# Output gate by tanh, and other places and load orders in the first projections of a hybrid mLSTM / MLA block

## The chip, the cores and the metric

One core of a Trainium2 chip runs the whole block in one launch. The metric is the device time in microseconds (us) of one execution; the median of several runs is given.

## The reference, cut to what matters

A sequence of 2048 tokens with 1024 features goes through one encoder layer. Beside the query and key columns the input projection gives the values, the output gate `o_pre`, the mLSTM gates, the compressed queries `c_q` (256 columns), the compressed keys `c_kv` (128) and the rotary keys (64).

```python
xn = rms_norm(h, ln_mix_g[l])
proj = xn @ w_in[l]
# mLSTM group: forward and backward chunkwise recurrence, then
h = rms_norm(h_fwd + h_bwd, norm_g)          # by head
y_a = sigmoid(o_pre) * h
# MLA group
q  = (rms_norm(c_q, q_norm_g) @ w_uq)        # 4 heads: 128 + 64 (rope)
kv = (rms_norm(c_kv, kv_norm_g) @ w_ukv)
y_b = softmax((q_nope k_nope^T + rope(q_rope) rope(k_rope)^T) * scale) @ v
h = h + concat(y_a, y_b) @ w_out             # then a conv-gated FFN, a gated
                                             # per-layer input and a final norm
```

## The kernel before, in words

The class `Block` runs the stages one after the other: the input projection (`in_proj`), attention with the mLSTM running beside it (`attend` over `mlstm`), the output projection, the FFN, the per-layer input and the final norm. All products are fp32 made of three fp32r passes: each operand is split into a high part (a cast on ScalarE, line 119) and a low part (a subtraction on VectorE, line 122), and `mm3` (line 132) multiplies high by high, high by low and low by high.

Tiles live in SBUF places with names: "w...", "x...", "t...", "s...". `self.at(place, ...)` puts a new tile into a place, and the first instruction that writes the new tile waits for the last reader of the old one. Only TensorE's order is written by hand. ScalarE, VectorE, GpSimd and SyncE get their order from a scheduler, and each works strictly in that order, so that an instruction that waits holds up all behind it. Almost all loads and stores are issued by SyncE (SP).

`in_proj` has three parts.

1. *The rest columns*, 0 to about 100 us: 16 row tiles `st` of 128 tokens. `load_x` (line 220) loads the transposed tile x_t, `load_rows` (line 225) the same rows untransposed, x_r, into two places in turn, for the sum of squares (`ssq_x`). `split_x` makes xh and xl; the product with the weights wsp gives 464 columns, from which come the gates gt (line 249, with the bias bg), the raw rows rs (line 252), the norms nn (lines 265 and 266, with gn) and the rows of compressed queries and keys, which are turned and stored in `rest_d` in DRAM. At `st` 10, `absorb_load` loads the turned up-projections of queries and keys into w8 and t6.
2. *The value columns*, about 100 to 263 us: 16 tiles of eight steps. A step is three matmuls, one with an xl and two with an xh (bk<-wsp,xl and bk<-wsp,xh). After each step `beside()` runs pieces of side work: the mLSTM gates in every third step, 1.4 pieces a step from the chain `absorb()` then `q_up()`, and from step 68 on every second step `raised`, which forms sums of x (xs, xsum) and splits them (op) for the third part.
   - `absorb()` multiplies the query up-projection by the key up-projection (gb<-ukvt,uqt), and for each head h the value up-projection by that head's 128 rows of w_out (gb<-woa,uvs); the result woo goes to `wo_d`. The raw rows wor have one place, w11; the next head's are loaded when this head's are split. There are six pauses (of one piece each) between split and product.
   - `q_up()` loads the compressed queries from `rest_d`, four of the eight column groups c of 256 tokens at a time (qraw, 1 MB, x11 and then x5), splits a group into cq in w8, multiplies by the up-projection (qpr<-wqo,cq for the rotary part, gb<-cq,wqn for the other), rotates (qtt, qro), splits (qsr) and turns (L788). w8 also holds the woo of `absorb`.
3. *Query, key and output-gate columns in pairs* (Winograd form), about 263 to 498 us. `finish()` applies Silu to the queries (line 582 for the convolved ones) and Sigmoid to the output gate (line 564, tiles uv and ug), and stores the gate in `o_d`.

`attend` starts within the last pair: score products into bk (lines 1135 to 1139), maxima (line 1140), exp (line 1158, pe), turning (line 1198, tb), and the split of the turned probabilities (pt). Exp and Sigmoid, and Exp and Silu, need different tables on ScalarE; a change is an ACT_TABLE_LOAD. The mLSTM beside it ends each chunk with line 1103: the turned tile (mb) times the output gate (og).

Of the kernel before, what the change touches and what calls it, by code (L numbers as in the profile page):

```python
# [11 lines left out]
F32R = mybir.dt.float32r  # L12
BF16 = mybir.dt.bfloat16
AF = mybir.ActivationFunctionType
ALU = mybir.AluOpType
# [4 lines left out]
P = 128  # L20
S = 2048
D = 1024
KT = D // P
NT = S // P
# [18 lines left out]
def pause(n):  # L43

    for _ in range(n):
        yield
# [14 lines left out]
class Block:  # L61
# [120 lines left out]
    def in_proj(self):  # L182
# [38 lines left out]
            return t  # L221

        def load_rows(st):
            t = self.at(("w13", "u2")[st % 2], [P, D], name="x_r")
            nc.sync.dma_start(t, d["x"][0, st * P:(st + 1) * P, :])
            return t

# [85 lines left out]
        with self.tc.manual_schedule(engines={ET.PE}):  # L313
            for st in range(NT + LAG_X + 1):
                if st + 2 < NT:
                    xq[st + 2] = load_x(st + 2)
                if st == 0:
                    rq[1] = load_rows(1)
                if st == 10:
                    self.absorb_load()  # L320
                if 14 <= st < 17:
                    vraw.append(load_raw(st - 14, OFF_V, 512, f"w{st - 4}"))
                if st == 0:
                    gn = self.at("t5", [P, 384], name="gn")
                    self.row_bcast(gn[:, 0:256], d["q_norm_g"][0], 256)
                    self.row_bcast(gn[:, 256:384], d["kv_norm_g"][0], 128)
                    bg = self.bg = self.row_bcast(self.cst.tile([P, 16], F32, name="bg"), d["b_gates"][0], 16)
                if 1 <= st < NT:
                    split_x(st, xq.pop(st))
                if 0 <= st - 1 < NT:  # L330
                    ssq_x(st - 1, rq.pop(st - 1))
                    if st + 1 < NT:
                        rq[st + 1] = load_rows(st + 1)
                if st == NT:
                    vws = split_raw(vraw[0], 512, VT)
                if 0 <= st - LAG_X - 1 < NT:
                    nq[st - LAG_X - 1] = norm_rest(st - LAG_X - 1, *sq.pop(st - LAG_X - 1))
                if 0 <= st - LAG_X < NT:
                    sq[st - LAG_X] = rest(st - LAG_X)
                if 0 <= st - LAG_X - 1 - LAG_R < NT:  # L340
                    turn_rest(st - LAG_X - 1 - LAG_R, nq.pop(st - LAG_X - 1 - LAG_R))

        cols = self.cst.tile([P, 8], F32, name="cols")
        self.gmix, ng = cols[:, 0:4], cols[:, 4:8]
        nc.sync.dma_start(self.gmix, d["gm_turned"])

        H = S // 2
        NAMES = ("B11", "T1", "T2", "B21", "T3", "T4", "B22")
# [52 lines left out]
            ws += split_raw(vraw[k2], 512, VT[2 * k2:])  # L401
        gates, raised = self.gates(), highs()
        side = chain(self.absorb(), self.q_up())
        when = [0, 0.0, False]

        def beside():

            n = when[0]
            when[0] += 1
            if n in (3, 8):  # L410
                turn_rest(NT - 2 + n // 8, nq.pop(NT - 2 + n // 8))
            if n >= 12 and n % 3 == 0:
                next(gates, None)
            if n >= 4:
                when[1] += self.VRATE
                while when[1] >= 1:
                    if next(side, self) is self and not when[2]:
                        when[2] = True
                        self.in_load(0)
                    when[1] -= 1  # L420
            if n == 10:
                pr = self.pml.tile([NT, P], F32, name="rps", tag="ml")
                nc.tensor.transpose(pr, rcol, self.ident)
                rr = self.at("s2", [NT, P], name="rrow")
                nc.vector.tensor_copy(rr, pr)
                nc.sync.dma_start(self.r_d.rearrange("(t p) -> t p", p=P), rr)
            if n >= 68 and n % 2 == 1 and (n < 82 or when[2]):
                next(raised, None)

        with self.tc.manual_schedule(engines={ET.PE}):  # L430
# [86 lines left out]
    def in_pairs(self, high, cwt, rrow, gcol, ng, row):  # L517
# [42 lines left out]
        def finish(s, half):  # L560
            u, c0 = (s.ug, s.uv)[half], 0 if s.i >= 6 else 8
            if s.kind == "o":
                t = u[:, 1:1 + H]
                nc.scalar.activation(t, t, AF.Sigmoid)
                dst = self.o_d[c0:c0 + 8, :, 2 * s.j + half, :]
            else:
                ct = s.j + 4 * half
                nc.vector.memset(u[:, 0:1], 0.0)
                if c0:
                    nc.vector.memset(u[:, H + 1:H + 2], 0.0)  # L570
                    nc.vector.tensor_copy(ehi[:, ct:ct + 1], u[:, 1:2])
                else:
                    nc.vector.tensor_copy(u[:, H + 1:H + 2], ehi[:, ct:ct + 1])
                    nc.vector.tensor_copy(elo[:, ct:ct + 1], u[:, H:H + 1])
                t = self.at(("w7", "w11")[half], [P, H], name="ct")
                nc.scalar.activation(t, u[:, 0:H], AF.Identity, bias=cwt[:, 3, ct:ct + 1], scale=cwt[:, 0, ct:ct + 1])
                for tap in (1, 2):
                    nc.vector.scalar_tensor_tensor(t, u[:, tap:tap + H], cwt[:, tap, ct:ct + 1], t,
                                                   op0=ALU.mult, op1=ALU.add)
                if c0:  # L580
                    nc.vector.tensor_copy(pa[:, ct:ct + 1], t[:, 0:1])
                nc.scalar.activation(t, t, AF.Silu)
                dst = self.qk_d[c0:c0 + 8, :, ct, :]
# [137 lines left out]
    def absorb(self):  # L721
# [9 lines left out]
            self.wqr.append(r)  # L731

        def load(h):
            r = self.at("w11", [P, D], name="wor")
            nc.sync.dma_start(r, d["w_out"][0, 512 + h * P:512 + (h + 1) * P, :])
            return r

        raw = load(0)
        yield from pause(5)
        for kt in range(2):  # L740
            ps = self.gbank([P, NH, P])
# [3 lines left out]
            yield  # L745
        for h in range(NH):
            wh, wl = [self.at(t, [P, D], F32R, "woa") for t in ("w12", "w10")]
            self.split(raw, wh, wl)
            if h + 1 < NH:
                raw = load(h + 1)  # L750
            us = self.at(f"s{h % 2}", [P, 2, P], F32R, "uvs")
            self.split(uv[:, h], us[:, 0], us[:, 1])
            yield from pause(6)
            o = self.at("w8", [P, D], name="woo")
            for hf in range(2):
                fs = slice(hf * 512, hf * 512 + 512)
# [7 lines left out]
    def q_up(self):  # L764
# [8 lines left out]
        raws, tables, old = {}, {}, None  # L773

        def load(c):
            raws[c // 4] = self.at(("x11", "x5")[c // 4], [P, 2, 1024], name="qraw")
            nc.sync.dma_start(raws[c // 4], self.rest_d[:, 0:2, c * 256:c * 256 + 1024])

        def table(c):
            tables[c // 2] = self.at(f"s{c // 2 % 3}", [P, 4, 2, 32], name="qcs")  # L780
# [18 lines left out]
        yield from pause(4)  # L799
        sr2 = self.at("x13", [P, 2, 2, NH, P], name="qsr")  # L800
        for c in range(8):
            cc = self.at("w8", [P, 2, 2, 256], F32R, "cq")
            o = c % 4 * 256
            self.split(raws[c // 4][:, :, o:o + 256], cc[:, 0], cc[:, 1])
            if c == 2:
                load(4)
            cs = tables[c // 2][:, c % 2 * 2:c % 2 * 2 + 2]
            ch, cl = cc[:, 0], cc[:, 1]
            yield from pause(1 if c else 7)
# [148 lines left out]
    def mlstm(self):  # L958
# [60 lines left out]
        for c in range(NT):  # L1019
# [80 lines left out]
            pt = mbank([P, NH, P])  # L1100
            for h in range(NH):
                nc.tensor.transpose(pt[:, h, :], hh[:, h, :], self.ident)
            nc.vector.tensor_tensor(hy[:, 1], pt, og, op=ALU.mult)
            nc.sync.dma_start(self.y_d[c, :, 0:4, :], hy[:, 1])
            yield

# [1056 lines left out]
```

## Time and profile before

| | |
|---|---|
| time before, median of 3 runs | 2942.8 us (2942.41 to 2944.44) |
| the profiled execution's own time | 2938.07 us |
| its span | 2936.1 us |
| mean granted TensorE clock | 0.995 |
| instructions | 40731 |
| moved by DMA | 530.19 MB, 181 GB/s on average |

How to read it: a line of the page or of a view gives the engine (PE is the matmul unit, PEld its weight loads, DVE VectorE, ACT ScalarE, POOL GpSimd, SP SyncE, SPq its DMA queue), the line of the kernel, the operation, the output and the inputs, the shape, and times in us. In brackets stands how long the engine was idle before, and what released it. PEclk is the clock granted to TensorE, 1.00 being full speed.

### The profile page before, as it was taken

Reading aid. Unit: us, or ns where it says so; the run is one execution under the profiler, and the core shown is the slowest. Engines: PE = TensorE matmul, PEld = TensorE weight load, DVE = VectorE, ACT = ScalarE, POOL = GpSimd, SP = SyncE. Lnnn points to the kernel's source line nnn. Section 1 sums busy time; section 2 is a strip of 40 time slices with the busy share of each in tenths; the row PEclk is TensorE's granted clock in tenths of the full one; section 3 lists DMA queues with packets and bytes.
Section 4 is the critical chain, followed back from the end, with each engine's and each line's share of the span. In section 5 each row is a group of like instructions: output and inputs, shape, how many; then the busy total and the mean of one; then the engine's idle time right before and its main releaser. Section 6 shows DMA issues by size and latency. Waiting matters only on the chain.

```text
span 2936.1 us, 40731 instructions
## 1 busy us (share of the span) xinstructions
PE 2860.6 (97%) x14543; PEld 2405.6 (82%) x14543; DVE 2099.5 (72%) x3724; ACT 1536.2 (52%) x2925; POOL 154.6 (5%) x295
## 2 busy tenths in 40 slices
PE   8889999999999999899999999999999999999998
PEld 7778887988988898788788887888887788878776
DVE  7555888777777787536778777777778766676776
ACT  7544566555655666423455555655556333244654
POOL 4100000000000000000000000000000000002011
PEclk9999999999999999999999999999999999999999
DMA  9756665443333343458645545657776667575864
GB/s 277 216 176 183 186 184 158 132 143 98 96 96 100 107 129 103 140 199 277 209 143 175 190 160 164 197 179 234 232 237 200 222 195 240 171 252 199 278 191 156
DMA packets 423850, 530.19 MB, mean 181 GB/s; under 512 B 31424, under 2 KB 285408, under 8 KB 423648
## 3 DMA queue, kind: packets, MB, share of 16 engines
q1 hardware_dynamic: 423648, 527.60, 56.3%
q8 instruction: 114, 1.87, 0.3%
q14 instruction: 88, 0.72, 0.1%
HBM read 347.49 MB, written 180.02 MB: 180 GB/s over the span
## 4 chain that ended last, share of the span: by engine, by line
PE 66%; DVE 6%; DMA 4%; ACT 4%; issue 3%; POOL 1%; SPq 0%; POOLq 0%; ACTq 0%; DVEq 0%
PE fxy L513 30%; PE fz L513 12%; PE ppv L132 5%; PE bk L132 3%; PE tb L1198 3%; PE bk L1135 2%; PE bk L1137 1%; PE bk L1139 1%; PE bk L1136 1%; PE bk L1138 1%; PE fs L132 1%; ACT pe L1158 1%; PE mb L1074 1%; PE mb L1075 1%; DMA opr<-tw_d 1%
## 5 line engine op out<-in xcount | busy, mean ns | idle before, releaser
L513 PE MATMUL fxy<-op,fw 128*128 128x512 f32 x3552 | 854.9, 393 | 18.2 <-DVE fh L1642 7.4
L513 PEld LDWEIGHTS fxy<-op,fw 128*128 128x128 f32 x3552 | 661.2, 188 | 175.7 <-DVE fh L1642 13.6
L513 PE MATMUL fz<-op,fw 128*128 128x512 f32 x1776 | 441.1, 391 | 5.3 <-DVE xt L1372 2.7
L513 PEld LDWEIGHTS fz<-op,fw 128*128 128x128 f32 x1776 | 333.0, 188 | 74.7 <-DVE xt L1372 2.9
L119 ACT CAST pt<-tb 128x512 fp32r<-128x512 f32 x256 | 147.2, 586 | 183.9 <-PE tb L1198 183.0
L513 PE MATMUL fxy<-op,fwd 128*128 128x512 f32 (+1 forms) x888 | 214.1, 389 | 1.0 <-ACT gate L1990 0.8
L1140 DVE TENSOR_REDUCE mx<-bk 128x1 f32<-128x512 f32 x255 | 174.4, 684 | 47.6 <-PE bk L1139 46.8
L132 PE MATMUL ppv<-pt,kv 128*128 128x256 f32 x1536 | 203.5, 287 | 0.0
L122 DVE TENSOR_TENSOR pt<-tb,pt 128x512 fp32r<-128x512 f32 x256 | 173.8, 683 | 32.1 <-ACT pt L119 31.2
L513 PEld LDWEIGHTS fxy<-op,fwd 128*128 128x128 f32 x888 | 165.2, 188 | 36.0 <-ACT gate L1990 1.2
L132 PEld LDWEIGHTS ppv<-pt,kv 128*128 128x128 f32 x1536 | 188.9, 191 | 0.3 <-ACT pt L119 0.3
L1158 ACT ACTIVATE pe<-bk,nm 128x512 f32<-128x512 f32 x255 | 173.9, 696 | 26.7 <-DVE nm L1152 25.8
L132 PE MATMUL bk<-wo,yhl 128*128 128x512 f32 x744 | 177.1, 396 | 5.9 <-DVE yhl L122 5.9
L132 PEld LDWEIGHTS bk<-wo,yhl 128*128 128x128 f32 x744 | 140.1, 190 | 35.0 <-DVE yhl L122 6.3
L132 PE MATMUL bk<-wsp,xh 128*128 128x464 f32 (+1 forms) x512 | 157.8, 390 | 0.2 <-DVE wsp L122 0.2
L1198 PE MATMUL tb<-ident,pe 128*128 128x128 f32 x1024 | 149.7, 273 | 4.6 <-DVE pt L122 4.3
L1198 PEld LDWEIGHTS tb<-ident,pe 128*128 128x128 f32 x1024 | 121.5, 140 | 24.2 <-DVE pt L122 6.0
L119 ACT CAST fw<-hraw 128x1024 fp32r<-128x1024 f32 (+1 forms) x72 | 70.3, 981 | 125.0 <-PE fxy L513 96.3
L1642 DVE TENSOR_TENSOR fh<-fh,fxy 128x512 f32<-128x512 f32 x95 | 65.1, 685 | 90.9 <-PE fxy L513 90.6
L122 DVE TENSOR_TENSOR fw<-fwr,fw 128x1024 fp32r<-128x1024 f32 x88 | 107.3, 1220 | 29.8 <-ACT fw L119 29.8
L1693 DVE SCALAR_TENSOR_TENSOR fgv<-uv,fcw,fgv 128x1024 f32<-128x1024 f32 x88 | 112.7, 1281 | 10.6 <-ACT fgv L1691 9.9
L119 ACT CAST op<-opr 128x512 fp32r<-128x512 f32 x153 | 89.1, 618 | 50.9 <-PE fxy L513 22.6
(431 smaller groups left out, 5064.2 us busy)
## 6 DMA issues: line engine op xcount, KB each, us to landing
fwr<-in_w_up SPq DMA_DIRECT2D x66, 512.0 KB, 4.9
fh<-h_d SPq DMA_DIRECT2D x48, 512.0 KB, 3.7
h_d<-fh SPq DMA_DIRECT2D x48, 512.0 KB, 4.9
s_d<-fwr SPq DMA_DIRECT2D x44, 512.0 KB, 2.7
fws<-s_d SPq DMA_DIRECT2D x44, 512.0 KB, 4.0
rw<-row_d SPq DMA_DIRECT2D x32, 512.0 KB, 4.8
tw_d<-tsum SPq DMA_DIRECT2D x60, 256.0 KB, 5.4
opr<-tw_d SPq DMA_DIRECT2D x60, 256.0 KB, 5.3
```

What stands on the lines that cost most here:

```text
L119: nc.scalar.copy(hi, src)
L122: (sub or nc.vector).tensor_tensor(lo, src, _f(hi), op=ALU.subtract)
L132: mm = lambda *a, **k: self.nc.tensor.matmul(*a, **k, skip_group_check=more)
L513: self.nc.tensor.matmul(out, a[:, k * P:(k + 1) * P], parts[lo][:, cols], start=first, stop=lo == 1 and k == last, skip_group_check=more)
L1074: mm(ps[:, i, 0:129], mk2[:, r, h, :], v1[:, h, :], start=True, stop=False)
L1075: mm(ps[:, i, 0:129], qi2[:, r, h, :], cst[r][:, h, :], start=False, stop=True)
L1135: mm(ps, ql, kh[:, ks], start=True, stop=False)
L1140: nc.vector.tensor_reduce(s.mx[:, kb:kb + 1], ps, axis=AX.X, op=ALU.max)
L1158: nc.scalar.activation(s.pe[:, kb % 2], s.banks[kb], AF.Exp, bias=s.nm, scale=ASCALE, accum_out=s.rs[:, kb:kb + 1])
L1198: nc.tensor.transpose(t[:, j, :], s.p[kb][:, j * P:(j + 1) * P], self.ident)
L1642: add = lambda o, a, b: tt(o, a, b, op=ALU.add)
L1693: nc.vector.scalar_tensor_tensor(t, u[:, tap:tap + 2 * SB], taps[:, tap, ct:ct + 1], t, op0=ALU.mult, op1=ALU.add)
```

## The change

- The output gate is Tanh of half its input in place of Sigmoid. The mixing gain `gmix` is halved, and line 1103 becomes (og + 1) times the turned tile, one instruction as before: sigmoid(x) = (1 + tanh(x/2)) / 2.
- `absorb()` keeps two heads' rows of w_out in flight: even heads in w11, odd ones as two halves in t1 and t2. The pauses between split and product are five, so that the four heads give four pieces fewer and all side work behind them is run some three steps earlier.
- `q_up()` loads column groups 0 to 3 as before (1 MB, x11) and 4 to 7 one by one (256 KB each, in t1, t2, t3 and t1 again), asked for at the splits of groups 0, 1, 2 and 4. The first cq lies in x10, the others in w8 as before.
- x_r has three places in turn up to tile 13, and a load of x_r is issued at the end of an iteration rather than ahead of or within it. `absorb_load` is called at `st` 14 rather than 10, since w8 is the third place.
- `raised` also waits until the gates' side work is done. The gates' last piece stands at step 51, ahead of step 68, so the order does not change by this.

```diff
         def load_rows(st):
-            t = self.at(("w13", "u2")[st % 2], [P, D], name="x_r")
+            t = self.at(("w13", "u2", "w8")[st % 3 if st < 14 else st % 2], [P, D], name="x_r")
...
-                if st == 0:
-                    rq[1] = load_rows(1)
-                if st == 10:
+                if st == 14:
                     self.absorb_load()
...
                     ssq_x(st - 1, rq.pop(st - 1))
-                    if st + 1 < NT:
-                        rq[st + 1] = load_rows(st + 1)
+                if st + 1 < NT:
+                    rq[st + 1] = load_rows(st + 1)
...
         nc.sync.dma_start(self.gmix, d["gm_turned"])
+        nc.vector.tensor_scalar(self.gmix, self.gmix, 0.5, None, op0=ALU.mult)
...
-                nc.scalar.activation(t, t, AF.Sigmoid)
+                nc.scalar.activation(t, t, AF.Tanh, scale=0.5)
...
         def load(h):
+            if h % 2:
+                r = [self.at(f"t{1 + i}", [P, 512], name="wor") for i in range(2)]
+                for i in range(2):
+                    nc.sync.dma_start(r[i], d["w_out"][0, 512 + h * P:512 + (h + 1) * P, i * 512:i * 512 + 512])
+                return r
             r = self.at("w11", [P, D], name="wor")
             nc.sync.dma_start(r, d["w_out"][0, 512 + h * P:512 + (h + 1) * P, :])
-            return r
-
-        raw = load(0)
+            return [r]
+
+        raws = [load(0), load(1)]
...
-            self.split(raw, wh, wl)
-            if h + 1 < NH:
-                raw = load(h + 1)
+            raw = raws.pop(0)
+            for i, r in enumerate(raw):
+                cs = slice(i * D // len(raw), (i + 1) * D // len(raw))
+                self.split(r, wh[:, cs], wl[:, cs])
+            if h + 2 < NH:
+                raws.append(load(h + 2))
...
-            yield from pause(6)
+            yield from pause(5)
...
         def load(c):
-            raws[c // 4] = self.at(("x11", "x5")[c // 4], [P, 2, 1024], name="qraw")
-            nc.sync.dma_start(raws[c // 4], self.rest_d[:, 0:2, c * 256:c * 256 + 1024])
+            n = 4 if c == 0 else 1
+            t = self.at("x11" if c == 0 else f"t{1 + (c - 4) % 3}", [P, 2, 256 * n], name="qraw")
+            nc.sync.dma_start(t, self.rest_d[:, 0:2, c * 256:(c + n) * 256])
+            for i in range(n):
+                raws[c + i] = t[:, :, i * 256:i * 256 + 256]
...
-            cc = self.at("w8", [P, 2, 2, 256], F32R, "cq")
-            o = c % 4 * 256
-            self.split(raws[c // 4][:, :, o:o + 256], cc[:, 0], cc[:, 1])
-            if c == 2:
-                load(4)
+            cc = self.at("w8" if c else "x10", [P, 2, 2, 256], F32R, "cq")
+            self.split(raws[c], cc[:, 0], cc[:, 1])
+            if c < 3:
+                load(4 + c)
+            if c == 4:
+                load(7)
...
-            nc.vector.tensor_tensor(hy[:, 1], pt, og, op=ALU.mult)
+            nc.vector.scalar_tensor_tensor(hy[:, 1], og, 1.0, pt, op0=ALU.add, op1=ALU.mult)
```

How the order of the instructions moves, at three places.

TensorE in the value stage, from the third step after the last one that reads xl01_126 (the tile whose place, x11, the first queries take) to the first query product. Before:

```order
L132 MATMUL bk_1718<-wsp_1392,xl10_127 128x512
L132 MATMUL bk_1718<-wsp_1392,xh10_119 128x512 x2
L132 MATMUL bk_1718<-wsp_1395,xl10_127 128x512
L132 MATMUL bk_1718<-wsp_1395,xh10_119 128x512 x2
L132 MATMUL bk_1718<-wsp_1398,xl11_128 128x512
L132 MATMUL bk_1718<-wsp_1398,xh11_120 128x512 x2
L132 MATMUL bk_1718<-wsp_1401,xl11_128 128x512
L132 MATMUL bk_1718<-wsp_1401,xh11_120 128x512 x2
L132 MATMUL qpr_1751<-wqo_1692,cq_1723 128x256 x12
```

And now, from the last step that reads xl01_126 itself:

```order
L132 MATMUL bk_1668<-wsp_1408,xl01_126 128x512
L132 MATMUL bk_1668<-wsp_1408,xh01_118 128x512 x2
L132 MATMUL bk_1733<-wsp_1239,xl10_127 128x512
L132 MATMUL bk_1733<-wsp_1239,xh10_119 128x512 x2
L132 MATMUL bk_1733<-wsp_1242,xl10_127 128x512
L132 MATMUL bk_1733<-wsp_1242,xh10_119 128x512 x2
L924 MATMUL gps_1740<-mg_1632,gtmp_1514 128x32
L132 MATMUL bk_1733<-wsp_1393,xl10_127 128x512
L132 MATMUL bk_1733<-wsp_1393,xh10_119 128x512 x2
L132 MATMUL qpr_1753<-wqo_1692,cq_1719 128x256 x12
```

Three steps stand between the last reader of xl01_126 and the first query product, where six stood: two steps with xl10_127 and a gates product (gps) precede the rows shown of before.

SyncE at the same place, where the queries (qraw) are loaded, the value rows (vo) and absorbed weights (woo) stored, the w_out rows (wor) and rope tables (qcs) loaded. Before:

```order
L735 DMA wor_1590<-in_w_out 128x1024
L781 DMA qcs_1703<-in_rope 128x4x64
L760 DMA wo_d_91<-woo_1644 128x1024
L781 DMA qcs_1705<-in_rope 128x4x64
L777 DMA qraw_1701<-rest_d_87 128x2x1024
L760 DMA wo_d_91<-woo_1678 128x1024
L439 DMA v_d_84<-vo_1715 128x512
```

And now:

```order
L791 DMA qcs_1703<-in_rope 128x4x64
L767 DMA wo_d_91<-woo_1635 128x1024
L785 DMA qraw_1722<-rest_d_87 128x2x256
L438 DMA v_d_84<-vo_1665 128x512
L785 DMA qraw_1820<-rest_d_87 128x2x256
L791 DMA qcs_1705<-in_rope 128x4x64
L785 DMA qraw_1942<-rest_d_87 128x2x256
L767 DMA wo_d_91<-woo_1678 128x1024
L785 DMA qraw_1701<-rest_d_87 128x2x1024
L438 DMA v_d_84<-vo_1730 128x512
```

The last w_out load is earlier (it stands above these rows now), three loads of 256 columns and the last store of woo stand ahead of the load of 1024 columns.

ScalarE where the last output gates (uv, ug) meet the first exp of attention. Before:

```order
L582 ACTIVATE ct<-ct 128x1024
L1158 ACT_TABLE_LOAD
L1158 ACTIVATE pe,rs<-bk,nm 128x512 x2
L564 ACT_TABLE_LOAD
L564 ACTIVATE uv<-uv 128x1024
L1158 ACT_TABLE_LOAD
L1158 ACTIVATE pe,rs<-bk,nm 128x512
L1158 ACTIVATE pe,rs<-sc_4577,nm 128x512
L564 ACT_TABLE_LOAD
L564 ACTIVATE ug<-ug 128x1024
L119 CAST pt<-tb 128x4x128 x2
L1158 ACT_TABLE_LOAD
```

And now:

```order
L581 ACTIVATE ct<-ct 128x1024
L1169 ACT_TABLE_LOAD
L1169 ACTIVATE pe,rs<-bk,nm 128x512 x2
L563 ACTIVATE uv<-uv 128x1024
L1169 ACTIVATE pe,rs<-bk,nm 128x512
L1169 ACTIVATE pe,rs<-sc_4592,nm 128x512
L563 ACTIVATE ug<-ug 128x1024
L119 CAST pt<-tb 128x4x128 x3
L985 COPY kk<-mb 128x512
```

The four table loads between the exps and the output gates are gone; one, ahead of the first exp, stays.

More of the change, by code (lines that the diff above doesn't have):

```diff
@@ L403, in in_proj @@
         side = chain(self.absorb(), self.q_up())
-        when = [0, 0.0, False]
+        when = [0, 0.0, False, False]
         def beside():
@@ L411, in beside @@
                 turn_rest(NT - 2 + n // 8, nq.pop(NT - 2 + n // 8))
-            if n >= 12 and n % 3 == 0:
-                next(gates, None)
+            if n >= 12 and n % 3 == 0 and next(gates, self) is self:
+                when[3] = True
             if n >= 4:
@@ L426, in beside @@
                 nc.sync.dma_start(self.r_d.rearrange("(t p) -> t p", p=P), rr)
-            if n >= 68 and n % 2 == 1 and (n < 82 or when[2]):
+            if n >= 68 and n % 2 == 1 and when[3] and (n < 82 or when[2]):
                 next(raised, None)
```

## The prediction

> **What bounds the kernel now.** I read the page first, then the busy time by stage, then TensorE's waits in the stages that the change touches.
>
> ```profile
> span 2936.1 us, 40731 instructions
> PE 2860.6 (97%) x14543; PEld 2405.6 (82%) x14543; DVE 2099.5 (72%) x3724; ACT 1536.2 (52%) x2925; POOL 154.6 (5%) x295
> ```
>
> TensorE (PE) is busy in 2860.6 of 2936.1 us. An edit on another engine can only give back a part of the other 75.5 us, and of the time in which PE runs at half clock. The busy time by stage (the window, its length, then PE, PEld, DVE, ACT, POOL, the granted clock, the DMA share and GB/s) tells where that is:
>
> ```profile
> 0.00:30.00 30.00, 20.61 (x80) 16.58 (x81) 17.86 (x43) 19.39 (x47) 6.68 (x18) 0.97 0.89 263
> 30.00:100.00 70.00, 70.00 (x354) 62.48 (x353) 54.97 (x195) 52.93 (x132) 40.49 (x66) 0.99 0.89 259
> 100.00:150.00 50.00, 42.12 (x194) 32.21 (x193) 24.43 (x71) 20.10 (x39) 1.14 (x3) 0.97 0.65 205
> 150.00:200.00 50.00, 43.10 (x271) 38.41 (x270) 26.57 (x66) 18.63 (x36) 0.00 (x0) 0.92 0.56 174
> 200.00:240.00 40.00, 38.15 (x239) 33.58 (x238) 26.69 (x53) 22.27 (x40) 0.00 (x0) 1.00 0.71 211
> 300.00:400.00 100.00, 100.00 (x441) 82.52 (x440) 84.18 (x134) 59.97 (x76) 0.00 (x0) 1.00 0.67 199
> 400.00:510.00 110.00, 107.15 (x482) 87.87 (x481) 88.03 (x148) 68.23 (x91) 0.00 (x0) 1.00 0.51 155
> ```
>
> PE lacks 7.9, 6.9 and 1.9 us in the value stage (100 to 240 us), 2.9 us in 400 to 510, and nothing in 30 to 100 and 300 to 400. What PE waited for (total, times, longest), from 0 to 100, 100 to 142, 142 to 240 and 484 to 512 us:
>
> ```profile
> PE bk L132 <- DVE xl L122: 2.3, 2, 1.8
> ...
> PE gb L132 <- DVE woa L122: 1.9, 3, 0.8
> PE gb L132 <- ACT woa L119: 1.3, 1, 1.3
> ...
> PE qpr L132 <- DVE cq L122: 9.9, 2, 5.6
> PE gb L788 <- DVE qsr L830: 1.9, 1, 1.9
> ...
> PE tb L1198 <- DVE pt L122: 1.9, 1, 1.9
> PE bk L1135 <- ACT pe L1158: 0.5, 1, 0.5
> ```
>
> The largest is the query product qpr, late twice for its operand cq. Its chain in time (start, length, engine, instruction, in brackets the idle time before and its releaser):
>
> ```profile
> 137.04 0.40 PE L132 MATMUL bk<-wsp,xl 128*128 128x512 f32 x1
> ...
> 137.47 0.38 SPq L777 DMA_DIRECT2D qraw<-rest_d  x1
> ...
> 137.73 0.39 PE L132 MATMUL bk<-wsp,xl 128*128 128x512 f32 x1
> ...
> 137.94 0.42 SPq L760 DMA_DIRECT2D wo_d<-woo  x1
> ...
> 145.14 0.62 ACT L119 CAST cq<-qraw 128x512 fp32r<-128x512 f32 x1 [6.52 <-DMA wo_d<-woo]
> ...
> 146.54 2.22 PE L132 MATMUL qpr<-wqo,cq 128*128 128x256 f32 x12 [4.31 <-DVE cq L122]
> ...
> 185.64 0.36 SPq L777 DMA_DIRECT2D qraw<-rest_d  x1
> ...
> 191.71 0.62 ACT L119 CAST cq<-qraw 128x512 fp32r<-128x512 f32 x1 [4.01 <-DMA qraw<-rest_d]
> ...
> 193.20 1.19 PE L132 MATMUL qpr<-wqo,cq 128*128 128x256 f32 x4 [5.56 <-DVE cq L122]
> ```
>
> Each megabyte of queries is asked for just before its use: 6.1 us pass from the second issue to the cast. Each wait is followed by half clock (same columns as by stage; three windows):
>
> ```profile
> 147.40:150.80 3.40, 3.40 (x15) 3.11 (x15) 1.93 (x5) 0.00 (x0) 0.00 (x0) 0.51 0.00 0
> 193.20:198.60 5.40, 5.40 (x22) 5.11 (x23) 3.54 (x8) 0.00 (x0) 0.00 (x0) 0.50 0.06 20
> 27.90:31.30 3.40, 3.40 (x10) 2.92 (x9) 2.47 (x7) 2.19 (x4) 2.18 (x4) 0.51 0.80 235
> ```
>
> Work at half clock takes twice as long: they cost 1.7, 2.7 and 1.7 us.
>
> **The change, part by part.** The sum is made against the profiled execution (2938.07 us, its span and 2.0 us around it). The median shown is 2942.8, 4.7 us more; I carry the difference over unchanged.
>
> *w_out, two loads in flight.* The waits for woa (1.9 + 1.3 = 3.2 us) come from one raw buffer. With two, the next row's data lies there when its split starts, and that split is queued one row ahead. The first split now comes one step nearer its product; I leave 0.2 us of wait: gain 3.0.
>
> *First qpr.* Its load goes into x11 when the last step that reads xl_126 ends. By the 3.0 us this moves from 137.47 to 134.5. I give the load the second one's 6.1 us: 140.6. From there to the product the first one took 146.54 - 145.14 = 1.4 us: 142.0. (The cast waited in before for the wo_d store to free w8; with cq in x10 it does not.) PE's side: it reached qpr at 146.54 - 4.31 = 142.23, 4.76 after the issue. Four pauses fewer put qpr three steps nearer (three steps stand between, not six). A step is 137.73 - 137.04 = 0.69 us, so PE arrives 4.76 - 2.07 = 2.7 us after the issue, at 137.2, and waits 4.8 instead of 4.31: loss 0.5. The half-clock window behind it stays. Bounds: three 256 KB loads and the wo_d store are queued just ahead and share the DMA engines, +3.5 us at the worst (the 6.1 taken half as long again); at the best the load lands 3 us sooner and the 1.7 of half clock goes too, a gain of 4.7.
>
> *Second qpr.* Columns 4 to 7 come in four loads into t1, t2, t3, t1; the first three are issued ahead of the first megabyte, some 50 us before the second stall's place. The wait of 5.56 and the 2.7 of half clock go: gain 8.3. The fourth load waits for the split of column 4 and is wanted three columns later. Between the two stalls four columns took 193.2 - 146.5 = 47 us, so it has over 30 us against the 6.1.
>
> *Raised sums.* DVE and ACT do the splits and sums of the value stage in one order; the sums' xs loads, and the xsum loads moved behind t1 to t3, can come late. The rows that show such a wait: qsr above (1.9) and this group (idle 1.9 for its DMA):
>
> ```profile
> L459 DVE SCALAR_TENSOR_TENSOR xs<-xs,gcol 128x512 f32<-128x512 f32 x4 | 3.0, 750 | 1.9 <-DMA xs<-in_x_turned 1.9
> ```
>
> I charge 1.0, half of one such wait; bounds 0 and 1.9 + 1.7 of half clock.
>
> *Start.* x_r of tile 1 is issued behind gn and bg:
>
> ```profile
> 21.10 0.36 DVE L249 SCALAR_TENSOR_TENSOR gt<-bk,rcol,bg 128x8 f32<-128x8 f32 x2 [0.24 <-DMA bg<-in_b_gates]
> ...
> 25.99 0.49 DVE L265 SCALAR_TENSOR_TENSOR nn<-rs,rsr,gn 128x256 f32<-128x256 f32 x1 [1.21 <-POOL rsr L142]
> ...
> 27.39 0.48 PE L132 MATMUL bk<-wsp,xl 128*128 128x464 f32 x1 [1.77 <-DVE xl L122]
> ```
>
> DVE reaches nn late because gt waited for bg; xl of the fourth tile stands behind nn and PE waits 1.77 for it. With bg earlier, gt goes ahead of the third tile's xl (two gt, 0.36 us, plus rounding: about 0.5 later there) and the fourth's xl waits no more: 1.77 - 0.5 = 1.3. Bounds: -0.5 (only the delay) and 2.6 (some of the half clock at 27.9 goes). The third x_r buffer and absorb_load four tiles later fall into 30 to 100 us, where PE has no gap: 0; they would cost only if DMA, at 0.89 there, made xl late.
>
> *Tanh for Sigmoid.* The o gate's table switches in 300 to 400 lie behind a PE that is never idle: 0. At the handover to attention they are not covered:
>
> ```profile
> 502.72 1.28 ACT L564 ACT_TABLE_LOAD   x1
> ...
> 504.01 1.06 ACT L564 ACTIVATE ug<-ug 128x1024 f32<-128x1024 f32 x1
> 504.98 1.05 ACT L119 CAST pt<-tb 128x512 fp32r<-128x512 f32 x2
> ...
> 506.05 1.28 ACT L1158 ACT_TABLE_LOAD   x1
> 506.41 1.22 PE L1198 MATMUL tb<-ident,pe 128*128 128x128 f32 x8 [1.90 <-DVE pt L122]
> ```
>
> Exp and Tanh stand in the order without a load between; here four loads go. PE's two waits there, 1.90 and 0.54, are all that can be won: 2.44. The 1.06 of the o gate itself stays ahead of pt: gain 1.4, bounds 0.5 and 2.44. The Trainium skill (ScalarE: Activation LUTs, "What ACT_TABLE_LOAD costs") counts 2.66 us a switch, 1.28 of load and 1.38 of drain. The trace has no drain: the Activate starts 1.29 us after the load. By the page more slack would come free, and the gain here would be the whole 2.44, the forecast 1.0 us lower.
>
> The new product replaces an operation of the same length:
>
> ```profile
> L1103 DVE TENSOR_TENSOR hy<-mb,og 128x512 f32<-128x512 f32 x16 | 10.9, 681 | 0.5 <-PE mb L1102 0.5
> ...
> L978 DVE SCALAR_TENSOR_TENSOR kk<-kk,cols 128x512 f32<-128x512 f32 x30 | 20.6, 686 | 6.1 <-DMA kk<-kn_d 4.3 <-ACT kk L974 1.2 <-DMA y_d<-ya 0.4
> ```
>
> 16 x 5 ns is 0.1 us on an engine that waits there; with the one small product on gmix: 0.
>
> Sum: 3.0 - 0.5 + 8.3 - 1.0 + 1.3 + 1.4 = 12.5. Profiled 2925.6; forecast 2942.8 - 12.5 = **2930.3 us**.
>
> **The rivals.**
> (a) *Only the gap moves.* The first megabyte sits behind the small loads and the store: its wait grows by the 3.5 above and runs into a second half-clock window (1.7), the raised sums cost 3.6, start and handover give nothing. 3.0 - 0.5 + 8.3 - 3.5 - 1.7 - 3.6 = 2.0: 2940.8. For it: DMA share 0.65 there. Against: the small loads are issued several us earlier.
> (b) *Raised sums late: slower.* The loads of the sums in 100 to 240 us (count, size, us from issue to landing):
>
> ```profile
> xs<-in_x_turned SPq DMA_DIRECT2D x8, 512.0 KB, 4.8
> ```
>
> If each of these eight, issued in order on SP behind the query stores and now met by a PE that is 10 us ahead, stops PE as qsr did (1.85 and a half-clock window, 1.7), that is 8 x 3.55 = 28.4: 2942.8 - 12.5 + 1.0 + 28.4 = 2959.7. It decides from six of eight (5.2 make it 0.2% slower). Against: in before the group waited 1.9 in all.
> (c) *The first wait goes as well.* The load lands early enough that less than 1.8 us remain and its clock window goes: 12.5 + 0.5 + 4.7 = 17.7, 2925.1. The Trainium skill (TensorE: Matmul & The Clock Gate, "Why this matters for your kernels") wants no gap over about 3 us between bursts. The trace has half clock after 4.31 and 5.56 as the page says, but also after 1.77. Were the page's bound the whole story, (c) would need only a wait below 3 us.
> (d) *It doesn't do what it says.* One small load is held on SP, so that column 4 still comes late: 12.5 - 8.3 = 4.2, 2938.6.
>
> **How the numbers follow.** A measurement tells about 0.2% (5.9 us) from no change. Chances: forecast 0.70, (c) 0.15, (a) and (d) together 0.11, (b) 0.04. Faster 0.85, same 0.11, slower 0.04. The bounds of the first qpr, start and handover put the ends at about 7 more and 6 less gain: 2923 to 2937.
>
> **What would show it.** In the changed profile: no wait of woa above 0.3; the first qpr stall near 4.8 with one half-clock window; none at column 4; no L564 loads at the handover and PE's next tb some 1.4 us earlier against the score products; PE's gap in the fourth tile under 0.6. Wrong would be: a new wait of PE above 2 us in 150 to 260, or a gap in 30 to 100.

## The result and the profile after

The changed kernel took 2929.1 us (median of 5 runs, 2926.03 to 2930.37) against 2942.8 for the kernel before (5 runs by then): ratio 0.9951, 95% interval 0.9936 to 0.9965. That is 13.7 us by the medians and 10 to 19 by the interval, where 12.5 was forecast. A second comparison, e5 below, gave 0.9973 (0.9962 to 0.9985), 8 us (4 to 11). The forecast gain lies between the two and above the second interval.

The profiled execution took 2930.37 us, 7.7 less than that of before. The page:

```profile
span 2928.6 us, 40726 instructions
PE 2860.5 (98%) x14543; PEld 2405.6 (82%) x14543; DVE 2098.0 (72%) x3727; ACT 1525.7 (52%) x2919; POOL 152.6 (5%) x295
```

PE is busy for the same 2860 us; the 7.5 us of span that are gone were idle time of PE. By stage (columns as in the prediction):

```profile
0.00:30.00 30.00, 22.01 (x93) 18.24 (x94) 18.42 (x45) 21.00 (x49) 8.88 (x20) 1.00 0.96 287
...
100.00:150.00 50.00, 42.39 (x199) 33.47 (x198) 24.37 (x72) 20.81 (x44) 1.14 (x3) 0.93 0.59 190
150.00:200.00 50.00, 48.98 (x324) 43.72 (x323) 29.47 (x71) 23.16 (x43) 0.00 (x0) 1.00 0.70 206
200.00:240.00 40.00, 37.38 (x203) 32.33 (x202) 28.01 (x51) 19.80 (x33) 0.00 (x0) 0.96 0.63 194
...
300.00:400.00 100.00, 98.82 (x434) 80.81 (x433) 81.77 (x133) 57.69 (x76) 0.00 (x0) 1.00 0.68 198
```

The window of 150 to 200 us filled up (43.10 to 48.98, clock 0.92 to 1.00). The first 30 us gained 1.4 of PE time, 100 to 150 hardly moved, and 300 to 400, which was full, now has a gap. TensorE's waits, in order of time (0 to 100, 100 to 142, 142 to 240, 360 to 410, 484 to 512 us):

```profile
PE bk L132 <- DVE xl L122: 1.2, 2, 0.8
...
PE gb L132 <- DVE woa L122: 1.5, 2, 0.8
PE gb L132 <- ACT woa L119: 1.1, 2, 0.6
...
PE qpr L132 <- DVE cq L122: 4.7, 1, 4.7
PE gb L798 <- DVE qsr L841: 2.6, 1, 2.6
...
PE tb L512 <- DVE ug L555: 1.1, 1, 1.1
...
PE bk L1146 <- ACT pe L1169: 1.0, 1, 1.0
```

One qpr wait is left of two (9.9 to 4.7). It is the first one, and its chain is the forecast's:

```profile
134.28 0.36 SPq L785 DMA_DIRECT2D qraw<-rest_d  x1
...
140.29 1.14 ACT L119 CAST cq<-qraw 128x512 fp32r<-128x512 f32 x2 [4.81 <-DMA qraw<-rest_d]
...
141.68 1.65 PE L132 MATMUL qpr<-wqo,cq 128*128 128x256 f32 x6 [4.69 <-DVE cq L122]
```

Issue 134.28 (forecast 134.5), 6.0 us to the cast (6.1), product at 141.68 (142.0), wait 4.69 (4.8). That the issue fell so near is luck: the forecast moved it by w_out's 3.0 us, and of the 3.2 us by which it moved, w_out's waits gave 0.6 and the start, which e4 below shows to be worth nothing, 2.3. What the forecast had not is the length of the half clock, which begins within this wait; this stretch of the changed kernel, and the one behind qsr's wait:

```profile
139.99:146.81 6.82, 5.13 (x21) 4.84 (x22) 3.35 (x8) 1.14 (x2) 0.00 (x0) 0.50 0.03 11
211.67:215.08 3.41, 3.41 (x14) 3.02 (x15) 1.01 (x2) 0.82 (x2) 0.00 (x0) 0.50 0.51 149
```

At a clock of 0.50 each costs half of PE's busy time in it: 2.6 and 1.7 us.

The start of the pair stage is the mark at which the value stage's parts can be read together. Here before, then the changed kernel:

```profile
264.44 1.98 PE L513 MATMUL bk<-xh,fw 128*128 128x512 f32 x8
```

```profile
256.14 1.98 PE L512 MATMUL bk<-xh,fw 128*128 128x512 f32 x8
```

8.3 us are won by there. From this mark to the last FFN product (fxy) the profiles of this case took between 2653.9 (e2 below) and 2666.3 us (e10), though the edits touch little of it: 2659.9 before, 2660.5 changed, 2665.2 in e4. So terms of 1 to 3 us are read from the waits and from this mark better than from the whole time. How much half clock lies ahead of the mark differs between executions too, so it is told apart from idle time below.

### The profile page after: what moved, and what is told of

It reads as the page before. It is cut to its first block, busy times and chain, and to the rows that moved or that the text cites. A ratio compares the mean times of both kernels' runs of the same rounds, so it can differ in the third digit from the quotient of the medians.

```text
span 2928.6 us, 40726 instructions
## 1 busy us (share of the span) xinstructions
PE 2860.5 (98%) x14543; PEld 2405.6 (82%) x14543; DVE 2098.0 (72%) x3727; ACT 1525.7 (52%) x2919; POOL 152.6 (5%) x295
## 4 chain that ended last, share of the span: by engine, by line
PE 78%; DVE 7%; DMA 6%; ACT 4%; issue 3%; POOL 1%; SPq 0%; POOLq 0%; ACTq 0%; DVEq 0%
PE fxy L512 30%; PE fz L512 12%; PE bk L132 7%; PE ppv L132 5%; PE bk L512 4%; PE tb L1209 3%; PE tb L512 2%; PE bk L1146 2%; PE bk L1148 2%; PE bk L1150 2%; PE bk L1147 2%; PE bk L1149 2%; PE fs L132 1%; PE mb L1085 1%; PE mb L1086 1%
## 5 line engine op out<-in xcount | busy, mean ns | idle before, releaser
L1146 PE MATMUL bk<-kv,q_s 128*128 128x512 f32 x255 | 114.4, 449 | 1.0 <-ACT pe L1169 1.0
```

What stands on the lines that cost most here:

```text
L1146: mm(ps, ql, kh[:, ks], start=True, stop=False)
```

## The experiments

The theory: nearly all of the gain is the second query stall (5.56 us and 2.7 of half clock), and the other parts each act only where TensorE waited. The rivals: the other terms of the forecast (w_out 3.0, start 1.3, Tanh 1.4) carry their share; or the stalls only move. Times are medians; ratios are to the kernel before on the same chip, with their intervals.

| run | time, us | before, us | ratio | pair stage begins, us |
|---|---|---|---|---|
| e1 Tanh alone | 2938.35 | 2942.14 | 0.9990 (0.9979 to 1.0000) | 268.52 |
| e2 query loads alone | 2932.71 | 2942.14 | 0.9967 (0.9957 to 0.9978) | 259.45 |
| e3 query loads and w_out | 2933.76 | 2942.14 | 0.9974 (0.9961 to 0.9986) | 255.40 |
| e4 start alone | 2943.14 | 2942.14 | 1.0005 (0.9995 to 1.0016) | 263.85 |
| e5 the change again | 2932.06 | 2940.32 | 0.9973 (0.9962 to 0.9985) | 255.35 |
| e6 first load split | 2930.53 | 2940.32 | 0.9963 (0.9950 to 0.9975) | 254.40 |
| e7 queries split, Tanh | 2926.18 | 2940.32 | 0.9951 (0.9938 to 0.9965) | 252.48 |
| e8 three pauses more | 2929.82 | 2940.32 | 0.9966 (0.9953 to 0.9978) | 252.97 |
| e9 first group early | 2924.71 | 2940.97 | 0.9949 (0.9934 to 0.9965) | 250.17 |
| e10 e9, gate store on ScalarE's queue | 2931.26 | 2940.97 | 0.9969 (0.9960 to 0.9978) | 252.08 |
| e11 Sigmoid again | 2932.29 | 2940.97 | 0.9972 (0.9962 to 0.9982) | 257.22 |
| e12 only the query loads, as in e9 | 2928.39 | 2939.51 | 0.9963 (0.9951 to 0.9976) | 250.72 |

**The parts by themselves.**

*e1*, the kernel before with the three lines of the output gate.

> The kernel before with only the output gate changed (Tanh of half the input, gmix halved, line 1103 as one instruction with +1). Theory (each part acts where TensorE waited): only the handover gives anything. TensorE's two waits there, 1.90 and 0.54 us, fall to about 1.0 together, as in the changed kernel; gain 1.4 us (0.5 to 2.4), 2941.4. Nothing at 300 to 400 us, where TensorE is busy 100.00 of 100. Rival (a switch costs more than its load, 2.66 us by the Trainium skill, and ScalarE also holds other waits): four switches at the handover and four ahead of it give 5 us or more, 2938 or less.

Its waits at 360 to 410 and at 484 to 512 us:

```profile
PE tb L514 <- DVE ug L557: 0.4, 1, 0.4
...
PE bk L1136 <- ACT pe L1159: 1.0, 1, 1.0
```

The handover's waits are 1.0 as expected, and a wait that before had not stands at tb. The time is 0 to 6 us lower, 2.9 by the ratio, so neither the theory nor the rival is excluded by it; e11 asks the same from the other side.

*e2*, the query loads of the change in the kernel before (`load(c)`, its calls, and the place of the first cq).

> The kernel before with only the query loads changed (column groups 4 to 7 singly into t1 to t3, first cq in x10). Theory: the second stall (5.56 us) and the half clock behind it (2.7) go, 8.3; the first stall also shortens, since cq no longer waits for the wo_d store (4.31 to about 3.2, with one half-clock window); w_out's waits stay at 3.2. Gain 9 (7 to 11), 2934. Rival (only the gap moves): the four small loads are late too, or the sums' loads behind them stop TensorE elsewhere by as much; gain under 4.

```profile
PE gb L132 <- ACT woa L119: 3.0, 2, 1.9
PE gb L132 <- DVE woa L122: 1.8, 3, 0.8
...
PE gb L791 <- DVE qsr L834: 3.1, 1, 3.1
PE qpr L132 <- DVE cq L122: 2.5, 1, 2.5
```

9.7 us (6.5 to 12.6): the theory's 9. The second stall is gone and the first is 2.5; of it qsr gives 1.2 back. By the mark this profile is only 5.0 us ahead of the one before: its waits for woa are longer too (4.8 against 3.2 us), and half clock costs it 6.7 us by there (6.1 before).

*e3*, e2 with `raws = [load(0), load(1)]` and `pause(5)`.

> As the run with the query loads alone, and the two w_out rows in flight with five pauses. Theory after the changed kernel's profile: woa's waits fall from 3.2 to about 2.6 only, since what is late is not the raw row but the cast on ScalarE, queued behind the copy of woo that waits for the store of the head before; three steps less stand ahead of the first query product, so its wait grows to about 4.7. Net to the run with the query loads alone: 0 to 1 us. Rival (the forecast's sum): 3.0 of woa's waits are won, net 2.5 us.

```profile
PE gb L132 <- ACT woa L119: 0.8, 1, 0.8
PE gb L132 <- DVE woa L122: 0.8, 1, 0.8
...
PE qpr L132 <- DVE cq L122: 5.5, 1, 5.5
```

woa's waits fell by 3.2 (4.8 to 1.6), more than the theory said, and the query wait grew by nearly as much, 3.0. The pair stage begins 4.05 us earlier than in e2, but 3.2 of that is half clock (3.5 us lost by there against 6.7), since here half of one stretch fell into the query wait. TensorE's idle time up to the mark is the same, 20.7 and 20.8 us: the stall moved. The time shows no gain (2933.8 to 2932.7).

*e4*, the start alone.

```diff
-            t = self.at(("w13", "u2")[st % 2], [P, D], name="x_r")
+            t = self.at(("w13", "u2", "w8")[st % 3 if st < 14 else st % 2], [P, D], name="x_r")
```

with the loads at the end of the iteration and `absorb_load` at tile 14.

> The kernel before with only the start changed (loads of x_r at the end of an iteration, a third place, absorb_load at tile 14). Theory: TensorE's wait at the fourth tile falls from 1.77 to 0.85 and the half clock behind it goes (1.7): the value stage begins about 2.3 us earlier; gain 2.3 (1.3 to 3), 2940.5. Rival (the half clock is a matter of the run's phase, not of the edit): gain 0.6 or less, and a half-clock window stands somewhere in 0 to 40 us.

```profile
PE bk L132 <- DVE xl L122: 0.8, 1, 0.8
PE rtp L280 <- DVE nn L274: 0.5, 1, 0.5
```

The theory's steps came in the profile, and its gain did not. The wait is 0.82 and there is no half clock ahead of 146.7 us, but the time is between 1.5 us faster and 4.7 slower. So the rival is right on the gain, though its window at 0 to 40 us is not there. The old start in another execution, e1, reads the same: one such wait, of 0.84 us.

With the old order of loads the fourth tile waited 1.77 (the profile of before), 0.84, 0.92, 1.71, 1.11 and 1.32 us, with the new one 0.82 to 0.92. Only the profile of before has half clock in the first 100 us. The first product of ukvt, a mark for the end of the rest columns, stands at 108.80 us there, at 106.0 to 107.3 in the five others with the old start, and at 106.5 to 108.0 in the eight with the new one. The profile of before had caught one of the longer waits and a clock window with it.

**The first query product.** *e5* is the changed kernel again, as the yardstick.

> The changed kernel once more, beside the next three on the same chip, as their yardstick. Theory: what the parts gave by themselves (query loads 9.7 us, Tanh 2.9, start nothing, w_out about nothing in the time) makes 10 to 14 us; 2929 to 2932 against the kernel before of the same chip at about 2942. In the profile: first query stall 4 to 5.5 us with one or two half-clock windows, none at column group 4. Rival (the 13.7 us of the first comparison were partly a lucky set of runs): under 9.

8 us (4 to 11): under the rival's 9, though the interval reaches the theory's 10. The first query wait is 4.9, the second is absent.

*e6*, the changed kernel with

```diff
-            nc.sync.dma_start(t, self.rest_d[:, 0:2, c * 256:(c + n) * 256])
+            for a, b in ((0, 1), (1, 4)) if n == 4 else ((0, 1),):
+                nc.sync.dma_start(t[:, :, a * 256:b * 256], self.rest_d[:, 0:2, (c + a) * 256:(c + b) * 256])
```

> The changed kernel with the first megabyte of queries asked for in two loads, 256 KB (column group 0) and 768 KB. Theory: the first query product waits for the landing of the whole megabyte (6.0 us from the issue to the cast in the changed kernel), and a quarter lands in about 3; the stall falls from 4.7 to about 1.7 and at least one half-clock window (1.7 us) goes: 3 to 6 us under the changed kernel. Rival (the fixed part of a load, or the three small loads and the store queued ahead, set the landing): the stall stays above 4 and the time does not move.

```profile
132.95 1.14 SPq L786 DMA_DIRECT2D qraw<-rest_d  x2
...
138.27 0.62 ACT L119 CAST cq<-qraw 128x512 fp32r<-128x512 f32 x1 [4.12 <-DMA qraw<-rest_d]
```

A quarter of the bytes took 5.3 us where the whole took 6.0 (changed kernel) and 6.3 (e5), and the wait was still 4.0; the time is 1.5 us under e5's, well within the intervals. The rival holds here: the bytes are worth 0.7 to 1.0 us, and e7 puts 2.4 us down to what is queued ahead.

*e7*, the kernel before with the query loads, the first split likewise, and Tanh.

> The kernel before with the query loads, the first of them split in two as above, and Tanh; w_out, its six pauses and the start as before. Theory: the first query product comes three steps later than in the changed kernel, so its stall, 2.5 us with the query loads alone, is gone or under 0.5 and has no half-clock window behind it; w_out's waits stay at 3 to 5 us; together within 2 us of the changed kernel with the split load. Rival (w_out in two buffers is worth its 3 us in the end): 3 or more slower than that.

```profile
138.66 0.38 SPq L780 DMA_DIRECT2D qraw<-rest_d  x1
...
141.59 0.62 ACT L119 CAST cq<-qraw 128x512 fp32r<-128x512 f32 x1 [1.77 <-DMA qraw<-rest_d]
...
143.27 1.59 PE L132 MATMUL qpr<-wqo,cq 128*128 128x256 f32 x12
```

The same 256 KB, with no small loads and no store right ahead, land in 2.9 us, and qpr does not wait. w_out's waits are 4.0 us, and the time is 4.4 us under e6's: the rival fell, and the theory's 2 us was too narrow, though the intervals of the two overlap.

*e8*, `pause(1 if c else 10)` in the changed kernel.

> The changed kernel with three pauses more ahead of the first query product (10 in place of 7), loads as in the changed kernel. Theory: the stall is the load's time less the steps that stand between; two to three steps of 0.69 us more cut 4.7 to about 2.7 to 3.3, and the work is done all the same: 1.4 to 2 us under the changed kernel, 3.4 if a half-clock window goes too. Rival (what is late is the cast on ScalarE or VectorE's queue, not the load): the stall stays at 4.7.

The wait stayed at 5.1, since this execution's megabyte took 7.8 us from issue (133.48) to cast (141.27), not 6.0; the cast was again released by the load, so the rival's queue is not the cause. The shorter stall of the theory did not come. The pair stage begins 2.4 us earlier than in e5, but 1.9 of that is half clock (1.5 us lost by there against 3.4), so what three steps more are worth stays open.

*e9*, group 0 of the queries in a place that is free earlier:

```diff
-            n = 4 if c == 0 else 1
-            t = self.at("x11" if c == 0 else f"t{1 + (c - 4) % 3}", [P, 2, 256 * n], name="qraw")
+            n = 4 if c == 1 else 1
+            t = self.at("x11" if c == 1 else f"t{c - 4 if c else 3}", [P, 2, 256 * n], name="qraw")
...
         load(0)
+        load(1)
```

(groups 5 to 7 are then loaded at the splits of 0 to 2).

> The changed kernel with column group 0 of the queries in t3 (256 KB, free well before x11), groups 1 to 4 as one load in x11 and 5 to 7 in t1, t2, t3. Theory: what makes the first query product late is that its load can only be asked for when x11 comes free, and then queues behind the small loads and a store (5.3 us for 256 KB with them, 2.9 without). Asked for some microseconds earlier, the wait of 4.9 and its 6.8 us of half clock (3.4 lost) go: the pair stage starts 5 to 8 us earlier than the 255 us of the changed kernel, and the time is 4 to 8 us lower. Rival (later waits for VectorE, at qsr, take the place): the pair stage starts at most 2 us earlier.

```profile
134.78 0.62 ACT L119 CAST cq<-qraw 128x512 fp32r<-128x512 f32 x1 [1.97 <-PE bk L132]
...
136.87 1.60 PE L132 MATMUL qpr<-wqo,cq 128*128 128x256 f32 x12
...
250.17 1.98 PE L512 MATMUL bk<-xh,fw 128*128 128x512 f32 x8
```

No wait and no half clock there; the pair stage begins 5.2 us before e5's, 3.5 of them less idle time of TensorE and 1.7 less half clock. It has the lowest median of all: 15 us (10 to 19) under the kernel before, though its interval overlaps the changed kernel's.

**Tanh.** *e10*, e9 with `(nc.scalar if s.kind == "o" else nc.sync).dma_start(...)` for the gate's stores.

> As the run with the first group early, and the output gate's stores to o_d issued by ScalarE in place of SP. With Tanh, TensorE has a new wait at tb<-op,fw about 388 us (0.44 to 2.55 us in six profiles, none in the kernels with Sigmoid). Theory: on SP the o_d store, which waits for the gate, now stands ahead of the loads of rrow and opr; with the store on another queue the wait falls under 0.5 us, gain 1 to 2 us. Rival (it is the loads themselves that are late, or VectorE): the wait stays at 1 to 2.5.

```profile
PE bk L512 <- ACT bk L602: 1.9, 1, 1.9
PE tb L512 <- DVE ug L555: 1.8, 1, 1.8
```

The theory fell: the wait stays at 1.8 with the store on another queue, one on ScalarE (1.9) comes with it, and the median is 6.6 us above e9's (the intervals just overlap). The rows of the changed kernel show what the wait hangs on:

```profile
386.12 2.65 ACT L119 CAST op<-opr 128x512 fp32r<-128x512 f32 x4 [4.25 <-DMA opr<-xn_d]
386.77 0.69 DVE L122 TENSOR_TENSOR op<-opr,op 128x512 fp32r<-128x512 f32 x1 [0.63 <-ACT op L119]
387.38 0.68 DVE L555 TENSOR_TENSOR ug<-ug,tb 128x512 f32<-128x512 f32 x1
...
388.11 2.11 PE L512 MATMUL tb<-op,fw 128*128 128x512 f32 x8 [1.11 <-DVE ug L555]
```

VectorE's L555, for which TensorE waits, stands behind a split of op whose load is late.

*e11*, the changed kernel with Sigmoid, gmix and line 1103 as before.

> The changed kernel with Sigmoid (and gmix and line 1103) as before. Theory: the handover's waits of TensorE go from 0.97 back to 1.7 to 2.4 us, but the wait at 388 us (1.1 to 2.6) goes: between 1.5 us faster and 1.5 us slower than the changed kernel, no difference that the times can tell. Rival (Tanh alone gave 2.9 us): about 3 us slower than the changed kernel.

Waits at 360 to 410 and 484 to 512 us:

```profile
PE bk L511 <- ACT bk L601: 0.2, 1, 0.2
...
PE tb L1208 <- DVE pt L122: 1.8, 1, 1.8
PE bk L1145 <- ACT pe L1168: 0.5, 1, 0.5
```

As the theory said: the handover loses 1.4 (2.3 against 0.97), the wait at tb is gone, and the time is the changed kernel's (0.9972 and 0.9973). Each interval is some 3 us wide to either side, so the rival's 3 us are not excluded.

This profile shows one thing more. SyncE's order at the query loads is the changed kernel's, and yet the first query product waits 8.07 us:

```profile
133.95 0.39 SPq L784 DMA_DIRECT2D qraw<-rest_d  x1
...
144.63 2.93 PE L132 MATMUL qpr<-wqo,cq 128*128 128x256 f32 x12 [8.07 <-DVE cq L122]
```

The megabyte took 9.3 us from issue to cast. In the five profiles that have the three small loads and a store ahead of the whole megabyte (changed kernel, e5, e3, e8, e11) this time was 6.0, 6.3, 6.8, 7.8 and 9.3 us; no run shows why it varies.

**What the rest is worth.** *e12*, the kernel before with nothing but the query loads in e9's order.

> The kernel before with nothing changed but the query loads, in the order of the run with the first group early (group 0 in t3, 1 to 4 in x11, 5 to 7 in t1, t2, t3; first cq in x10). w_out's one buffer, six pauses, Sigmoid and the start are as before. Theory: both query stalls go; w_out's waits (3.2 to 4.8 us in the profiles with one buffer, 1.0 to 2.6 with two) stay, and Tanh and the start are worth nothing that the times can tell; so 11 to 13 us under the kernel before and 2 to 4 above the run with the first group early. Rival (w_out's two buffers and Tanh are worth their terms of the forecast, 3.0 and 1.4, and the stalls come back elsewhere): under 9 us faster than before.

```profile
PE gb L132 <- DVE woa L122: 2.6, 4, 0.8
PE gb L132 <- ACT woa L119: 1.3, 2, 0.9
...
250.72 1.98 PE L513 MATMUL bk<-xh,fw 128*128 128x512 f32 x8
```

11 us (7 to 14), as the theory said. The pair stage begins only 0.55 us after e9's. e9 wins 2.0 at w_out (waits of 1.9 against 3.9 us); it gives 0.75 of that back at qsr and the products beside it (waits of 4.94 against 4.19 us in 142 to 240) and 0.2 in the start; for the rest TensorE is busier by the mark (234.23 us against 233.76), for a reason that is open. Query loads alone, in a better order, do what the whole change did, as far as the intervals tell.

## Why the prediction was right, point by point

The main step, the second query stall, was right and is shown by e2 and e12. That the sum of all terms came so near to 13.7 us was luck: the second comparison gave 8, and most of the other terms were wrong in size or cause.

- **Second query stall, 8.3.** Right, and it carried the forecast: gone in every kernel with the small loads, and alone worth 9.7 us (6.5 to 12.6) with what the first stall gained in e2. Rival (d) did not come.
- **First query stall, -0.5.** The wait was right in the two profiles of the changed kernel (4.69, in e5 4.94), but the 6.1 us given to the load stand at the low end of the 6.0 to 9.3 that were measured. "The half-clock window behind it stays" failed: 6.8 us of half clock stand there in both profiles where 3.4 stood, and cost 2.6 and 2.1 us (half of 5.13 and 4.13 of work) in place of 1.7. The bound of the small loads and the store queued ahead was real: 5.3 us with them (e6) and 2.9 without (e7) for the same 256 KB. Of rival (a), the second window came in both profiles and the longer wait in e11 (8.07, 3.3 above the forecast), but not its time of 2940.8. Rival (c) did not come; e9 shows that its gain was there, by asking earlier. (Two sums slip here: half of 6.1 is 3.05, not the 3.5 of (a), and (c)'s 17.7 counts the 0.5 twice, since the 3.0 within its 4.7 starts from the wait of 4.8.)
- **w_out, 3.0.** Mis-sized. The waits were 3.2 to 4.8 us in six profiles with one buffer (4.0 on average) and 1.0 to 2.6 in eight with two (1.9): 2.1 us less. In e3 the query wait took it back. The step that failed is that a second buffer brings the raw data in time and that nothing else is late. In the changed kernel the first head's row, which a second buffer cannot help, is still late: its cast waited 3.15 us for the load, and TensorE 1.4 us for woa. The other 1.2 us are the third head's. Its cast stood on ScalarE behind the copy of woo, which waited for the store of the head before:

```profile
121.28 1.07 ACT L766 COPY woo<-gb 128x512 f32<-128x512 f32 x2 [3.20 <-DMA wo_d<-woo]
...
122.23 1.06 ACT L119 CAST woa<-wor 128x1024 fp32r<-128x1024 f32 x1
...
123.34 0.49 PE L132 MATMUL gb<-woa,uvs 128*128 128x512 f32 x1 [0.43 <-ACT woa L119]
```

- **Raised sums, -1.0.** Sign right, size too small: qsr's wait went from 1.85 to 2.62 and took a half-clock window, 2.5 us in this profile. The mechanism was another than late loads: VectorE had work without a break from 205.0 to 211.4 us, and sums of x stood between the rotation and qsr:

```profile
206.59 0.75 DVE L458 SCALAR_TENSOR_TENSOR xs<-xs,gcol 128x512 f32<-128x512 f32 x1
...
210.78 0.69 DVE L841 TENSOR_TENSOR qsr<-qro,qsr 128x512 fp32r<-128x512 f32 x1
...
211.62 1.06 PE L798 MATMUL gb<-ident,qsr 128*128 128x128 f32 x4 [2.62 <-DVE qsr L841]
```

  The prediction named a new wait above 2 us in 150 to 260 us as a sign of being wrong; this one is not new, but it grew past that. Rival (b), eight such stops, did not come. (Its 5.2 stops for 0.2% leave out the 1.0 that its own sum takes back; with it they are 4.9.)
- **Start, 1.3.** Wrong in cause: the edit is worth nothing that e4 shows. The term rested on one execution's 1.77 us, where other executions with the same start had 0.84 to 1.71. Its rows say otherwise too: nn waited 1.21 us for rsr from GpSimd, and gt only 0.24 for bg. And 30 to 100 us, put at 0, got a wait of rtp for nn (0.5 to 0.8 us) in all eight profiles with the new start, where one of six with the old start has it. That the changed kernel's profile looked 2 us better at 108 us was the same chance.
- **Tanh, 1.4 and 0.** The handover was right (2.44 to 0.97, and 2.3 back in e11; 1.7 to 2.4 in the six profiles with Sigmoid, 1.0 to 1.2 in the eight with Tanh). The prediction had no term for half clock behind these waits: it stands there in three of the six with Sigmoid (e3, e11, e12; 1.6, 3.1 and 1.7 us) and in none with Tanh. The zero at 300 to 400 us was wrong: "PE is never idle" said nothing on the new order of the loads and splits there. 0.44 to 2.55 us of wait came at that product in all eight profiles with Tanh and in none with Sigmoid. Net: nothing that the times settle (0 to 6 us in e1, none in e11). Why the scheduler's order is worse there is not settled; the gate's store, the only cause that was tried, is not it alone. The Trainium skill's drain of 1.38 us beside a table load (ScalarE: Activation LUTs, "What ACT_TABLE_LOAD costs") showed nowhere: with Sigmoid back in e11 a load starts at 494.98, 0.03 us behind the end of ScalarE's instruction before it, and the next Activate at 496.27, 1.29 us after the load's start.

Up to the start of the pair stage the two profiles differ by 8.3 us, and the terms as read there give 7.4 of them: start 2.3 (the same product of ukvt stood at 108.80 and at 106.48 us), w_out 0.6, first stall -0.4 and -0.9 of clock, second 8.3, qsr -2.5. Behind it Tanh's 1.5 - 1.1 do not show: the part from there to fxy is 0.6 us longer in the changed kernel. The medians differ by 13.7 and by 8.3, since the profiled execution of before was a quick one (2938.07, the lowest run of that comparison 2940.54) and that of the changed kernel the slowest of its five (2930.37). The range and the sign were carried by the one term of 8.3; the smaller terms were within the spread and partly offset each other. Of the signs listed, the second stall and the gate's table loads are gone as said; the waits for woa (0.8, not 0.3), the second half-clock window and the gap in the fourth tile (0.85, not 0.6) are not as said.

## What to carry to other kernels

Where a load is asked for when its place comes free just ahead of its use, the place is the fault: find one that is free earlier for the first piece and ask for the rest singly. Look for the same wait in several executions before an edit is priced on it; here 1.77 us of one profile were 0.8 to 1.7 in others. An edit that only takes instructions off one engine still gives the scheduler a new order elsewhere, and its price has to be read there too.

## What the runs showed of the hardware

Half clock comes in windows of 3.41 us, and within one execution their starts lie whole windows apart: in the changed kernel at 139.99, 211.67 and 628.09 us, that is 21 and 122 windows from one to the next. The length of a wait alone does not say what follows: 4.31, 4.37 and 5.12 us (before, e4, e8) brought one window, 3.78, 4.69 and 4.94 (e1, changed kernel, e5) two, 2.92 and 2.98 (e3 and e11, at qsr) none, and 2.62 and 2.73 (changed kernel and e9, at qsr) one. How a wait falls into the windows is the likely reason; no run tests it alone. The Trainium skill (TensorE: Matmul & The Clock Gate, "What's actually happening") says that the window runs freely, 3413 ns long, and the traces agree; the rule of about 3 us of idle time in its "Why this matters for your kernels" does not hold here as a bound, by the waits at qsr just named.
